# A two-layer encoder trunk on one core: the second layer's output projection in seven half-depth products, and six plain tiles at the start

## The chip, the cores and the metric

The kernel runs on one core of one Trainium2 chip. The metric is the device time of one execution in microseconds (us). A kernel is timed several times, and the median is given. Profiles come from one profiled execution, which has a time of its own.

## The reference

The input x is 2048 positions by 1024 channels in float32. The first (even) layer projects the normalised x to 6144 channels, makes a short convolution branch and a recurrent branch (RG-LRU, both directions) from them, and projects back. The second (odd) layer is a gated linear attention (GLA) with four heads, in both directions. The end of it is what the change touches:

```
h = rmsnorm(x, norm_pre)
q, k, v, r, lr = split(h @ w_in)
o = gla(q, k, v, g) + flip(gla(flip(q), flip(k), flip(v), flip(g_b)))   # 4 heads of 256 values
o = rmsnorm(o, head_norm_g)                                             # over each head's 256 values
y = (o * silu(r)) @ w_out                                               # 1024 x 1024
x = x + rmsnorm(y, norm_post)
```

## The kernel before, in words

Activations lie transposed: channels on the 128 partitions, positions along a row. The 2048 positions are cut into four chunks of 512 (CH). A product in near float32 accuracy takes three float16 matmuls: each operand is split into a high half (a copy to float16, on ACT) and a low half (operand minus high half, on DVE), and weight high times operand high, weight high times operand low and weight low times operand high are added up in PSUM. These are the three lines that stand together everywhere: 774 to 776 for the first layer's input projection, 1103 to 1105 for its output projection, 1492 to 1494 for the second layer's input projection, 2034 to 2036 for the second layer's output projection. The helpers act (line 250), stt (254) and tt (258) issue all the work of ACT and DVE, and dma (279) issues every DMA from SP's queue, in order.

*Seven products.* A product over depth 256 for 256 outputs can be made from seven products over half the depth and for half the outputs, in place of eight, from sums of operands made ahead (Strassen's scheme in Winograd's form). The kernel uses this for most of the first layer's input projection (two weight tiles as a pair, with operands H and with weights that DVE combines and splits) and for the second layer's input projection. In the first layer, the tiles in the list `first` are computed plainly, eight half-depth parts each, because the combined operands aren't there yet at the start; all others are in `pairs`.

*The order of the work.* The kernel is written as generators, "threads", which a planner (class Order, line 56) steps through while the program is built. Each step says which engine it uses and how long it should take; the planner keeps a clock for each engine, tile pools with caps, and priorities, and appends the instructions to each engine in the order that its clocks give. The chip then runs each engine's list strictly in that order. A change of a cost, a cap or a priority so moves many instructions. SBUF is kept in 23 slots of 8 KB a partition, with a cap for each role (H, YC, WO2, YC2, ZB and so on), PSUM in eight banks.

*The first stage.* x is loaded and normed (line 508 holds its ones product, which sums over partitions), the weights arrive in raw tiles, are split or combined (wsplit, line 429) into pieces, and PE works through `first` and then `pairs`. Beside it DVE makes the convolution of the recurrent branch in UA and splits it into UH, which the gate products (lines 944 to 946) read.

*The end of the second layer.* The GLA goes head by head (scores, states and outputs, lines 1797 to 1891). Behind each head, gpost norms its output o by chunks in the order 1, 2, 0, 3 (CORD): ACT squares, DVE adds, a ones product (line 456) sums, and the root is taken. The gate silu(r), made by ACT into DQ and kept in DRAM as rd, is loaded into YL, and gpost_out (line 1959) multiplies. High and low halves of y go to DRAM as yod, 256 KB each, and come back as YC2 tiles of four such pieces (yc2_loader, line 2013). The weights odd_wo come at the end as raw tiles of 512 KB and are split by wq_split (line 1998) into WO2. bg_wq (line 2038) then computes the projection for five blocks (three of 512 positions and two of 256): for each of eight groups of 128 outputs, eight parts of the depth, three matmuls each. For the first block four banks are filled side by side, one depth part after another, since operands arrive one by one. post_odd (line 2086) norms each block, adds x (ZX) and writes it out. In the trace the buffer numbers are left out, and both kinds of WO and YC tiles carry the names WO and YC.

Of the kernel before, what the change touches and what calls it, by code (L numbers as in the profile page):

```python
# [13 lines left out]
ALU = mybir.AluOpType  # L14
# [143 lines left out]
def trunk_kernel(ctx: ExitStack, tc: tile.TileContext, xT, w_in, gate_w, w_out, odd_w, lr_w, lr_gw, odd_wo, params, outT):  # L158
# [12 lines left out]
    S.pool("raw", ["raw0", "raw1", "hv0", "hv1"])  # L171
# [4 lines left out]
        XC=8, TMP=2, H=NH, PC=2, XA=1, UA=1, UH=1, R=1, I=1, T=3, A=1, G=2, U=3, Z=2, YH=1,  # L176
        WO=8, YC=6, YB=2, XR=4, H2=3, LM=1, WV=4, V=2, VD=2, XS=1, QS=2, E=4, SB=1, O=2, DQ=2, YL=2,
        WO2=4, YC2=4, ZB=2, ZX=2))
# [152 lines left out]
    def lam_consts():  # L331
# [23 lines left out]
        nc.vector.tensor_scalar(out=gsc[:, 8:16], in0=par[:, C_OPOST:C_OPOST + 8], scalar1=-2.0 ** -25, scalar2=None,  # L355
# [15 lines left out]
    def w_loader(items):  # L371
        for key, src in items:
            w = W[key]
            w.raw = yield from wget("raw", [128, 8, 128], F32)
            yield from dma(w.raw.t, src, 512 * 1024)
            done(w.evr)
# [220 lines left out]
    first = [("xa", 0), ("gc", 0), ("xb", 0), ("zb", 0)]  # L597
    pairs = [(("gb", 0), ("xa", 1))]
# [13 lines left out]
    for c in range(1, 7):  # L612
        GWAFT[("xa", c + 1)] = [c + 1]
    ev_proj = Ev()

    def even_loader():
        for i, key in enumerate(order):
# [6 lines left out]
            for c in GWAFT.get(key, ()):  # L624
                w = W["gw", c]
                w.raw = yield from wget("raw", [128, 512], F32)
                yield from dma(w.raw.t, gate_w[c], 256 * 1024)
                done(w.evr)

# [36 lines left out]
    def w_split_pairs():  # L666
        for pair in pairs:
# [27 lines left out]
            for key in pair:  # L695
                yield from gw_split(key)
        retire()
# [145 lines left out]
    def bg_even():  # L843
        bs, evs = [], []
        for key in first:
# [5 lines left out]
        for p in range(2):  # L851
            for i, key, hf in [(i, key, hf) for i, key in enumerate(first) for hf in range(2)]:
# [5 lines left out]
                if p == 1 and hf == 1:  # L858
                    done(evs[i])
        for c in range(1, NCH):  # L860
# [197 lines left out]
    def wo_loader():  # L1058
        for ki in range(16):
            WR[ki] = yield from wget("raw", [128, 1024], F32)  # L1060
            r0 = krow(ki)
            yield from dma(WR[ki].t, w_out[r0:r0 + 128, :], 512 * 1024)
            done(evWR[ki])
# [230 lines left out]
    for key, _ in items_odd:  # L1294
        W[key] = Wt()
    WU = {}
# [27 lines left out]
    def w_prep():  # L1324
# [13 lines left out]
        done(evLRP)  # L1338
        for u in UNITS:
            prs = ukeys(u)  # L1340
            for i, pr in enumerate(prs):
                ra, rb = W[pr[0]], W[pr[1]]
                tmp = yield from pget()
                s = f32(tmp)

                evo = [Ev() for _ in range(7)]

                def op(j, src, evo=evo, u=u, i=i, last=i == len(prs) - 1):
                    p = yield from pget()
                    yield from wsplit(p, src)  # L1350
                    S.spawn(w_save(u, j, i, p, last), 3)
                    done(evo[j])

                def close(ra=ra, rb=rb, evo=evo):
                    yield ("w", evo[0])
                    yield ("w", evo[4])
                    wput(ra.raw)
                    yield ("w", evo[5])
                    yield ("w", evo[6])
                    wput(rb.raw)  # L1360

                yield ("w", ra.evr)
                yield ("w", rb.evr)
                a11, a12 = ra.raw.t[:, 0:4], ra.raw.t[:, 4:8]
                a21, a22 = rb.raw.t[:, 0:4], rb.raw.t[:, 4:8]
                S.spawn(op(0, a11), 3)
                S.spawn(op(2, a12), 3)
                yield from tt(s, a21, a22, ALU.add)
                S.spawn(op(1, s), 3)
                S.spawn(op(5, a22), 3)  # L1370
                yield from tt(a21, a11, a21, ALU.subtract)
                S.spawn(op(6, a21), 3)
                yield ("w", evo[1])
                yield from tt(s, s, a11, ALU.subtract)
                S.spawn(op(3, s), 3)
                yield ("w", evo[2])
                yield from tt(a12, a12, s, ALU.subtract)
                S.spawn(op(4, a12), 3)
                S.spawn(close(), 3)
                yield ("w", evo[3])  # L1380
                pput(tmp)
            if u == UNITS[0]:
# [10 lines left out]
                done(evWZd)  # L1393
        done(evPrep)

    evPrep = Ev()
    evRaw = Ev()

    def w_save(u, j, i, p, last):
        d = wu_d[u, j]  # L1400
        yield from dma(d[:, :, :, i * 128:i * 128 + 128] if u[0] == "v" else d, p.t, 256 * 1024)
        pput(p)
        if last:
            done(evWD[u, j])
# [356 lines left out]
    def gla(hd):  # L1761
# [3 lines left out]
        yield ("w", evWVd)  # L1765
        xs = yield from get("XS", [128, 16, 128])
# [4 lines left out]
        sfb = yield from get("SB", [128, 8, 256])  # L1771
        O[hd] = o
# [143 lines left out]
    evPost = [Ev() for _ in range(4)]  # L1916

# [36 lines left out]
    def y_out(i, c, sl, y, yl):  # L1954
        yield from dma(yo_d[i][:, :, sl], y, 256 * 1024)
        count(("yl", i // 2, c), 2, lambda: put(yl))
        done(evYO[i, c])

    def gpost_out(hd, o, tp, evR, evG, YL, evYL):
        for p, c in enumerate(CORD):  # L1960
# [3 lines left out]
            yv = YL[c].t[:, 1024:2048].bitcast(F16).rearrange("p (e a t) -> p e a t", e=2, a=2)  # L1964
            for et in range(2):
                i = 2 * hd + et
# [6 lines left out]
                y = yv[:, et]  # L1973
                yield from act(y[:, 0], ot, AF.Copy, scale=16.0)
                yield from stt(y[:, 1], ot, 16.0, y[:, 0], ALU.mult, ALU.subtract)
                S.spawn(y_out(i, c, sl, y, YL[c]), 1)
        wput(tp)
        for s in o:
            put(s)
# [238 lines left out]
```

## Time and profile before

| | before |
|---|---|
| median of 3 | 2230.99 us (2228.64 to 2232.93) |
| the profiled execution | 2228.18 us |
| its span | 2226.4 us |
| mean granted TensorE clock | 0.989 |
| PE / DVE / ACT busy | 2142.4 / 1518.4 / 1254.4 us |
| moved by DMA | 443.88 MB, 199 GB/s over the span |

The span runs from the first instruction to the last; the execution's own time is 1.8 us longer. PE is TensorE's matmuls, PEld its weight loads, DVE, ACT and SP the vector, scalar and sync engines; POOL does next to nothing here. A row of a timeline gives the start, the duration, the engine, the line, the instruction, its output and inputs, and in brackets the time that the engine idled before it with what it waited for. The duration of a matmul covers its way through the array; the distance between two starts is what it costs.

### The profile page before, as it was taken

To read this page: it belongs to the slowest core of one execution; us is meant where nothing else is said; L and a number is where in the kernel's file an instruction comes from. 1 tells how busy PE (TensorE), PEld (TensorE's weight loads), DVE (VectorE), ACT (ScalarE), POOL (GpSimd) and SP (SyncE) were. 2 spreads that over 40 slices of the span, in tenths; PEclk is the share of its full clock that TensorE was granted. 3 is DMA by queue.
4 is the path that set the end of the run, shared out by engine and by line. 5 is a ranking of instruction groups with operands and counts; after the bars stand their busy time and mean duration, and the time that the engine had idled before them with its cause. 6 is when DMAs were issued, how large, how long until landed. Compare 5 with 4: busy or idle time off the path is not lost.

```text
span 2226.4 us, 27957 instructions
## 1 busy us (share of the span) xinstructions
PE 2142.4 (96%) x11290; PEld 1151.8 (52%) x11290; DVE 1518.4 (68%) x1720; ACT 1254.4 (56%) x1636; POOL 2.8 (0%) x8
## 2 busy tenths in 40 slices
PE   5979999999999999999999999999999999997997
PEld 4434444444444444444444444778566666674446
DVE  7987887888687777774476775766447475667435
ACT  5557776877777675663443334376355555655322
POOL 0000000000000000000000000000000000000000
PEclk9999999999999999999999999999999999998999
DMA  7354443543544545469566576256746667456533
GB/s 266 147 222 175 173 181 147 194 186 136 223 152 180 203 151 205 164 242 334 175 183 218 191 287 235 115 207 247 275 179 235 252 223 297 172 188 219 170 112 114
DMA packets 155057, 443.88 MB, mean 199 GB/s; under 512 B 39856, under 2 KB 76848, under 8 KB 121136
## 3 DMA queue, kind: packets, MB, share of 16 engines
q1 hardware_dynamic: 154928, 442.10, 54.4%
q8 instruction: 88, 1.44, 0.3%
q14 instruction: 41, 0.34, 0.0%
HBM read 325.40 MB, written 116.65 MB: 199 GB/s over the span
## 4 chain that ended last, share of the span: by engine, by line
PE 78%; DVE 10%; DMA 6%; ACT 3%; issue 2%; SPq 1%; DVEq 0%; ACTq 0%
PE ps L774 15%; PE ps L776 15%; PE ps L775 15%; PE ps L1103 3%; PE ps L1104 3%; PE ps L1105 3%; PE ps L2034 2%; PE ps L2036 2%; PE ps L2035 2%; PE ps L1829 2%; PE ps L1492 2%; PE ps L1494 2%; PE ps L1493 2%; DVE H L258 2%; DMA raw<-odd_w 1%
## 5 line engine op out<-in xcount | busy, mean ns | idle before, releaser
L774 PE MATMUL ps<-H,hl 128*128 128x512 f16 (+1 forms) x896 | 337.5, 377 | 14.2 <-ACT H L250 5.2
L775 PE MATMUL ps<-H,hl 128*128 128x512 f16 (+1 forms) x896 | 337.4, 377 | 4.3 <-DVE H L258 4.3
L776 PE MATMUL ps<-H,hl 128*128 128x512 f16 (+1 forms) x896 | 337.3, 376 | 3.9 <-DVE hl L254 3.7
L774 PE MATMUL ps<-H,PC 128*128 128x512 f16 (+1 forms) x752 | 283.4, 377 | 4.2 <-DMA H<-hd 3.2
L776 PE MATMUL ps<-H,PC 128*128 128x512 f16 (+1 forms) x752 | 283.3, 377 | 0.6 <-DVE PC L254 0.6
L775 PE MATMUL ps<-H,PC 128*128 128x512 f16 (+1 forms) x752 | 283.3, 377 | 0.0
L1103 PE MATMUL ps<-YC,WO 128*128 128x512 f16 x512 | 194.9, 381 | 0.0
L1104 PE MATMUL ps<-YC,WO 128*128 128x512 f16 x512 | 194.8, 380 | 0.0
L1105 PE MATMUL ps<-YC,WO 128*128 128x512 f16 x512 | 194.6, 380 | 0.0
L775 PEld LDWEIGHTS <-hl 128*128 128x128 f16 x896 | 88.4, 99 | 113.2 <-issue 15.0
L776 PEld LDWEIGHTS <-hl 128*128 128x128 f16 x896 | 88.4, 99 | 112.0 <-issue 7.0
L774 PEld LDWEIGHTS <-hl 128*128 128x128 f16 x896 | 88.5, 99 | 103.3 <-issue 3.9
L1492 PE MATMUL ps<-WV,H 128*128 128x256 f16 x448 | 122.1, 273 | 1.8 <-ACT VD L250 1.8
L1493 PE MATMUL ps<-WV,H 128*128 128x256 f16 x448 | 122.1, 273 | 0.0
L1494 PE MATMUL ps<-WV,H 128*128 128x256 f16 x448 | 122.1, 273 | 0.0
L774 PEld LDWEIGHTS <-PC 128*128 128x128 f16 x752 | 73.6, 98 | 93.3 <-DMA H<-hd 6.6
L2034 PE MATMUL ps<-YC,WO 128*128 128x512 f16 (+1 forms) x320 | 110.0, 344 | 10.5 <-DMA YC<-yod 10.5
L776 PEld LDWEIGHTS <-PC 128*128 128x128 f16 x752 | 73.6, 98 | 87.9 <-DVE PC L254 0.9
L775 PEld LDWEIGHTS <-PC 128*128 128x128 f16 x752 | 73.6, 98 | 86.8 <-issue 0.3
L150 ACT ACT_TABLE_LOAD x89 | 114.2, 1283 | 1.6
L2036 PE MATMUL ps<-YC,WO 128*128 128x512 f16 (+1 forms) x320 | 110.2, 344 | 0.0
L2035 PE MATMUL ps<-YC,WO 128*128 128x512 f16 (+1 forms) x320 | 109.8, 343 | 0.0
(234 smaller groups left out, 4159.5 us busy)
## 6 DMA issues: line engine op xcount, KB each, us to landing
H<-hd SPq DMA_DIRECT2D x112, 1024.0 KB, 6.1
H<-gd SPq DMA_DIRECT2D x56, 1024.0 KB, 8.9
raw<-w_in SPq DMA_DIRECT2D x48, 512.0 KB, 4.4
yd<-YH SPq DMA_DIRECT2D x16, 1024.0 KB, 4.9
YC<-yd SPq DMA_DIRECT2D x64, 256.0 KB, 5.7
hd<-H SPq DMA_DIRECT2D x14, 1024.0 KB, 5.5
gd<-H SPq DMA_DIRECT2D x14, 1024.0 KB, 4.7
raw<-odd_w SPq DMA_DIRECT2D x24, 512.0 KB, 5.2
```

The lines of the kernel that those rows point to most:

```text
L774: nc.tensor.matmul(b.t[:, sl], lhsT=wh, rhs=hi, start=s, stop=False, skip_group_check=True)
L775: nc.tensor.matmul(b.t[:, sl], lhsT=wh, rhs=lo, start=False, stop=False, skip_group_check=True)
L776: nc.tensor.matmul(b.t[:, sl], lhsT=wl, rhs=hi, start=False, stop=e, skip_group_check=True)
L1103: nc.tensor.matmul(b.t, lhsT=wh, rhs=hi, start=start, stop=False)
L1104: nc.tensor.matmul(b.t, lhsT=wh, rhs=lo, start=False, stop=False)
L1105: nc.tensor.matmul(b.t, lhsT=wl, rhs=hi, start=False, stop=stop)
L1492: nc.tensor.matmul(b.t[:, i], lhsT=hi, rhs=wh, start=st, stop=False, skip_group_check=True)
L1493: nc.tensor.matmul(b.t[:, i], lhsT=hi, rhs=wl, start=False, stop=False, skip_group_check=True)
L1494: nc.tensor.matmul(b.t[:, i], lhsT=lo, rhs=wh, start=False, stop=e, skip_group_check=True)
L2034: nc.tensor.matmul(out, lhsT=wh, rhs=hi, start=start, stop=False)
L2035: nc.tensor.matmul(out, lhsT=wh, rhs=lo, start=False, stop=False)
L2036: nc.tensor.matmul(out, lhsT=wl, rhs=hi, start=False, stop=stop)
```

## The change

Four things are changed.

1. **First stage.** `first` has six tiles, with ("gb", 0) and ("xa", 1) added, and `pairs` one pair fewer. The raw pool has a third tile, and loads of weights are issued without waiting for the one before to land.
2. **Weights of the last projection.** odd_wo is loaded in the first stage, two row blocks at a time (a head's 256 rows), behind four of the pairs. `prep` makes eight operands of each: seven for the seven products and one that the plain products need. They are split as other weights are and saved to DRAM (wq_d, eight tensors of 1 MB). Before head 3's GLA outputs, wq_loader loads them, one into each of eight WO2 slots.
3. **Operands.** y_ops makes the seven operands of each head and chunk from y (four for chunk 3), high and low halves of 128 by 256 each, in place in the YL tile. Those of heads 0 to 2 go to DRAM as one tensor for a head and chunk (128 by 3584 in float16; 128 by 2048 for chunk 3) and come back into YC2 slots. Those of head 3 stay in the YL tile, which the products read.
4. **Products.** Three chunks of 512 are computed by wq_seven: seven products, each for two pairs of output groups, four heads of depth, 256 columns. The first of them begins with products 0 to 2 of heads 0 to 2; head 3's part of these follows, then products 3 to 6. ACT and DVE add the results up into ZB. The last chunk is computed plainly from the operands that are halves of y and of the weights themselves. The blocks' norms and outputs are separate threads.

```
-    first = [("xa", 0), ("gc", 0), ("xb", 0), ("zb", 0)]
-    pairs = [(("gb", 0), ("xa", 1))]
+    first = [("xa", 0), ("gc", 0), ("xb", 0), ("zb", 0), ("gb", 0), ("xa", 1)]
+    pairs = []
...
-        WO2=4, YC2=4, ZB=2, ZX=2))
+        WO2=8, YC2=3, ZB=4, ZX=2))
...
+    WOAFT = {pairs[6 + 3 * h][1]: [h] for h in range(4)}
...
+                for hd in WOAFT.get(key, ()):
+                    yield from prep(W["wo", 2 * hd], W["wo", 2 * hd + 1], save_q(hd), True)
...
+    def prep(ra, rb, save, out=False):
+        tmp = yield from pget()
+        s = f32(tmp)
...
+        def op(j, src):
+            p = yield from pget()
+            yield from wsplit(p, src)
+            S.spawn(save(j, p), 3)
+            done(evo[j])
...
+    def y_ops(hd, c, o, yl):
...
+        def split(j, src):
+            yield from act(yv[:, j, 0], src, AF.Copy, scale=4.0)
+            yield from stt(yv[:, j, 1], src, 4.0, yv[:, j, 0], ALU.mult, ALU.subtract)
+            done(ev[j])
...
+        if hd == 3:
+            YC2[c, 3] = yl
+            done(evYC2[c, 3])
+        else:
+            S.spawn(y_out(hd, c, yl), 1)
...
     def wq_loader():
+        yield ("w", evGet3)
+        for j in range(8):
+            yield ("w", evWQd[j])
+            WQ[j] = yield from get("WO2", [128, 4, 2, 512], F16)
+            S.spawn(fetch(WQ[j].t, wq_d[j], 2 ** 20, evWQ[j]), 4)
...
     def yc2_loader():
+        yield ("w", evGet3)
+        for c in CORD:
+            for h in range(3):
+                yield ("w", evYO[h, c])
+                s = yield from get("YC2", [128, T])
...
+        def product(j, mb, hs):
...
+            yield ("w", evWQ[j])
+            for h in hs:
+                yield ("w", evYC2[c, h])
...
+            for i in range(2):
+                for h in hs:
+                    wq3(bk[b, mb].t[:, i], j, h, 2 * mb + i, yop(c, h, j), new and h == 0 and i == 0, h == 3)
...
+        if blk == 0:
+            for j in range(3):
+                for mb in range(2):
+                    yield from product(j, mb, (0, 1, 2))
+            for j in range(3):
+                for mb in range(2):
+                    yield from product(j, mb, (3,))
+        for j in range(3 if blk == 0 else 0, 7):
+            for mb in range(2):
+                yield from product(j, mb, (0, 1, 2, 3))
```

wq3 issues the three matmuls (lines 2096 to 2098 of the changed kernel), yop picks operand j of a head.

The change also moves instructions, since the planner places everything anew. On DVE in the first stage, before the change, UH (the low half of the convolved input, UA) stands at row 119 of DVE's list, and the first gate product at row 1015 of PE's, where a matmul and a weight load have a row each. H holds the operands of the input projection, XC is x.

```order
L258 TENSOR_TENSOR XC_420<-XC_481,XC_420 128x2048
L254 SCALAR_TENSOR_TENSOR UA_1011<-XA_253,par,UA_1011 128x2046
L258 TENSOR_TENSOR H_1042<-XC_420,H_1042 128x4x512
L254 SCALAR_TENSOR_TENSOR UA_1011<-XA_253,par,UA_1011 128x2047
L258 TENSOR_TENSOR H_1061<-XC_443,H_1061 128x4x512
L254 SCALAR_TENSOR_TENSOR UA_1011<-XA_253,par,UA_1011 128x2047
L258 TENSOR_TENSOR U_259<-U_259,G_256 128x2048
L254 SCALAR_TENSOR_TENSOR UH_1096<-UA_1011,UH_1096 128x2048
```

In the changed kernel the same place on DVE reads as follows; hl and raw are weights.

```order
L258 TENSOR_TENSOR H_1095<-XC_436,H_1095 128x4x512
L258 TENSOR_TENSOR H_1125<-XC_459,H_1125 128x4x512
L258 TENSOR_TENSOR hl_265<-raw_630 128x512
L254 SCALAR_TENSOR_TENSOR UA_1183<-XA_269,par,UA_1183 128x2046
L254 SCALAR_TENSOR_TENSOR UA_1183<-XA_269,par,UA_1183 128x2047 x2
L254 SCALAR_TENSOR_TENSOR hl_265<-raw_598,hl_265 128x512
L254 SCALAR_TENSOR_TENSOR UH_1217<-UA_1183,UH_1217 128x2048
```

UH is now at row 120 of DVE's list, and the first gate product at row 1255 of PE's, 120 matmuls and as many weight loads later.

On PE at the passage from head 3's GLA to the projection, before the change, the last outputs of the GLA (lines 1889 and 1891) are followed by the projection (YC and WO).

```order
L1889 MATMUL ps_15053<-XS_14490,V_14309 128x128
L1891 MATMUL ps_15053<-E_14304,SB_14493 128x128
L2034 LDWEIGHTS WO_1403_15074
L2034 MATMUL ps_14995<-YC_1402_15073,WO_1403_15074 128x512
L2035 LDWEIGHTS WO_1403_15074
L2035 MATMUL ps_14995<-YC_1402_15073,WO_1403_15074 128x512
```

In the changed kernel three pieces of the same passage are these: the last GLA outputs (lines 1924 and 1926) and a product of heads 0 to 2 behind them; the ones product (line 455) of head 3's second chunk, which stands among such products; and the first product that reads head 3's YL.

```order
L1924 MATMUL ps_15400<-XS_14725,V_14571 128x128
L1926 MATMUL ps_15400<-E_14566,SB_14728 128x128
...
L2098 MATMUL ps_15424<-YC_1333_14859,WO_1337_14918 128x256
L455 MATMUL ps_15403<-hv_15416,ones_r 128x512 x2
L2096 LDWEIGHTS WO_1337_14918
L2096 MATMUL ps_15450<-YC_1325_14800,WO_1337_14918 128x256
...
L2098 MATMUL ps_15450<-YC_1333_14859,WO_1337_14918 128x256
L2096 LDWEIGHTS WO_1334_14885
L2096 MATMUL ps_14989<-YL_15264,WO_1334_14885 128x256
```

The six products of heads 0 to 2 stand at rows 18297 to 18557 of PE's list, between parts of head 3's GLA, and the ones product of head 3's first chunk at row 18395, ahead of the last GLA outputs.

On SP, where the last loads before the second block of the projection stand, before the change the operands come in pieces of 256 KB, mixed with stores of head 3's y.

```order
L279 DMA yod_248<-YL_15135 256x1x512
L279 DMA YC_1422_15262<-yod_241 128x2x512
L279 DMA yod_247<-YL_15198 256x1x512
L279 DMA YC_1422_15262<-yod_242 128x2x512
L279 DMA yod_248<-YL_15198 256x1x512
L279 DMA YC_1422_15262<-yod_243 128x2x512
L279 DMA YC_1422_15262<-yod_244 128x2x512
```

In the changed kernel the same place has the last two weight loads (WO from wqd), the gates of head 3 for two chunks (YL from rd) and then the second block's operands (YC from yod), three tensors, one for each of heads 0 to 2.

```order
L279 DMA WO_1346_14991<-wqd_144 128x4096
L279 DMA WO_1347_14992<-wqd_145 128x4096
L279 DMA YL_15264<-rd_231 128x2x512
L279 DMA YL_15267<-rd_232 128x2x512
L279 DMA YL_15425<-rd_231 128x2x512
L279 DMA YL_15453<-rd_232 128x2x512
L279 DMA YC_1427_15801<-yod_251 128x3584
L279 DMA YC_1429_15803<-yod_255 128x3584
L279 DMA YC_1430_15804<-yod_259 128x3584
```

YC_1427 takes the slot of YC_1325, which the first block's products read up to PE's row 18997, and YC_1429 another slot that is read up to row 19015, the block's last matmul. On PE that matmul, the ones product of this block's norm and the second block's first matmul follow each other.

```order
L2098 MATMUL ps_15233<-YL_15264,WO_1346_14991 128x256
L455 MATMUL ps_15834<-hv_15828,ones_r 128x512 x2
L2096 LDWEIGHTS WO_1334_14885
L2096 MATMUL ps_15802<-YC_1427_15801,WO_1334_14885 128x256
L2097 LDWEIGHTS WO_1334_14885
L2097 MATMUL ps_15802<-YC_1427_15801,WO_1334_14885 128x256
```

Nothing else stands on PE between the two blocks.

More of the change, by code (lines that the diff above doesn't have):

```diff
@@ L859, in bg_even @@
                     done(evs[i])
+        for key in first[4:]:
+            yield from plain(key, 0)
         for c in range(1, NCH):
@@ L1295, in trunk_kernel @@
         W[key] = Wt()
+    wq_d = [drams.tile([128, 4, 2, 512], F16, tag=f"wq{j}", name=f"wqd{j}") for j in range(8)]
+    evWQd = [Ev() for _ in range(8)]
     WU = {}
@@ L1338, in w_prep, with save_u, save @@
         done(evLRP)
+        def save_u(u, i, last):
+            def save(j, p):
+                d = wu_d[u, j]
+                yield from dma(d[:, :, :, i * 128:i * 128 + 128] if u[0] == "v" else d, p.t, 256 * 1024)
+                pput(p)
+                if last:
+                    done(evWD[u, j])
+            return save
         for u in UNITS:
@@ L1341, in w_prep @@
             for i, pr in enumerate(prs):
[L1342 to L1381, printed above, removed]
+                yield from prep(W[pr[0]], W[pr[1]], save_u(u, i, i == len(prs) - 1))
             if u == UNITS[0]:
@@ L1972, in gpost_out @@
                 yield from tt(ot, g, ot, ALU.mult)
[L1973 to L1976, printed above, removed]
+            S.spawn(y_ops(hd, c, o, YL[c]), 2)
         wput(tp)
-        for s in o:
-            put(s)
+        if hd == 3:
+            S.pools["slot"]["caps"].update(YC2=6)
         done(evPost[hd])
-    yo_d = [drams.tile([128, 2, T], F16, tag=f"yo{i}", name=f"yod{i}") for i in range(8)]
@@ L1983, in trunk_kernel @@
-    evYO = {(i, c): Ev() for i in range(8) for c in range(NCH)}
+    yo_d = [[drams.tile([128, 2 * T], F16, tag=f"yo{h}{c}", name=f"yod{h}{c}") for c in range(NCH)] for h in range(4)]
+    evYO = {(h, c): Ev() for h in range(4) for c in range(NCH)}
     WQ = {}
     evWQ = [Ev() for _ in range(8)]
-    WQR = {}
-    evWQR = [Ev() for _ in range(8)]
     def wq_loader():
-        yield ("w", evRaw)
-        for k in range(8):
-            WQR[k] = yield from wget("raw", [128, 1024], F32)
-            yield from dma(WQR[k].t, odd_wo[k * 128:(k + 1) * 128, :], 512 * 1024)
-            done(evWQR[k])
@@ new lines, in yop, with wq3 @@
+    def yop(c, h, j):
+        return YC2[c, h].t.bitcast(F16).rearrange("p (j a t) -> p j a t", j=8, a=2)[:, j]
+    BLK = [(512, 512), (1024, 512), (0, 512), (1536, 256), (1792, 256)]
+    evF = {(b, m): Ev() for b in range(len(BLK)) for m in range(8)}
+    FB = {}
+    def wq3(out, j, h, m, y, start, stop):
+        wh, wl = [WQ[j].t[:, h, a, m * 128:(m + 1) * 128] for a in range(2)]
+        hi, lo = y[:, 0], y[:, 1]
+        nc.tensor.matmul(out, lhsT=wh, rhs=hi, start=start, stop=False, skip_group_check=True)
+        nc.tensor.matmul(out, lhsT=wh, rhs=lo, start=False, stop=False, skip_group_check=True)
+        nc.tensor.matmul(out, lhsT=wl, rhs=hi, start=False, stop=stop, skip_group_check=True)
@@ L2038, in bg_wq, with zb_get @@
+    ZB = {}
+    evZB = [Ev() for _ in range(len(BLK))]
+    def zb_get():
+        yield ("w", evGLA[3])
+        for blk, (t0, n) in enumerate(BLK):
+            ZB[blk] = []
+            for _ in range(2):
+                s = yield from get("ZB", [128, 4, n])
+                ZB[blk].append(s)
+            done(evZB[blk])
     def bg_wq():
@@ L2112, in post_odd, with out_dma @@
-            put(tmp)
+                for k in range(4):
+                    yield from stt(x[:, k], y[:, k], gsc[:, 8 + hf * 4 + k:9 + hf * 4 + k], x[:, k], ALU.mult, ALU.add)
+            else:
+                yield from tt(x, x, y, ALU.add)
+            S.spawn(out_dma(blk, hf, x), 0)
+            put(yb[hf])
+        put(tmp)
+    def out_dma(blk, hf, x):
+        t0, n = BLK[blk]
+        c = t0 // CH
+        yield from dma(outT[hf * 4:hf * 4 + 4, :, t0:t0 + n].rearrange("k p t -> p k t"), x, 2048 * n)
+        count(("zx", c, hf), CH // n, lambda: put(ZX[c, hf]))
```

295 lines of the change are left out of this document (186 added, 109 removed).

## The prediction, made before the run

> **What bounds the kernel now.** I read the page first, for the engines' shares and the costliest groups.
>
> ```profile
> PE 2142.4 (96%) x11290; PEld 1151.8 (52%) x11290; DVE 1518.4 (68%) x1720; ACT 1254.4 (56%) x1636; POOL 2.8 (0%) x8
> ...
> L2034 PE MATMUL ps<-YC,WO 128*128 128x512 f16 (+1 forms) x320 | 110.0, 344 | 10.5 <-DMA YC<-yod 10.5
> ```
>
> PE is busy for 2142.4 of 2226.4 us, so all its idle time is 84.0 us, and whatever gains more than that must take away matmuls. The busy time by stage says where the 84 lie. The columns are the stretch, its length, then busy time (and count) of PE, weight loads, DVE, ACT and POOL, the granted clock, the DMA share and GB/s.
>
> ```profile
> 0.00:56.00 56.00, 31.75 (x213) 22.93 (x214) 41.92 (x64) 33.15 (x38) 0.79 (x6) 0.94 0.73 264
> 56.00:112.00 56.00, 53.72 (x240) 24.16 (x240) 55.73 (x45) 31.01 (x29) 0.00 (x0) 1.00 0.37 151
> 112.00:168.00 56.00, 42.88 (x191) 18.73 (x189) 47.45 (x69) 31.00 (x37) 0.00 (x0) 0.91 0.56 217
> 168.00:1000.00 832.00, 831.67 (x3853) 376.75 (x3852) 644.88 (x629) 593.85 (x652) 0.00 (x0) 1.00 0.48 180
> ...
> 2020.00:2040.00 20.00, 13.10 (x63) 7.82 (x62) 13.44 (x24) 12.22 (x20) 0.00 (x0) 0.83 0.77 252
> 2040.00:2060.00 20.00, 14.63 (x50) 5.95 (x50) 19.42 (x27) 12.31 (x18) 0.00 (x0) 0.84 0.80 260
> 2060.00:2200.00 140.00, 140.00 (x780) 76.42 (x779) 58.90 (x61) 40.31 (x75) 0.00 (x0) 1.00 0.41 141
> 2200.00:2226.40 26.40, 14.18 (x124) 12.05 (x121) 15.09 (x21) 7.23 (x20) 0.00 (x0) 0.83 0.23 80
> ```
>
> From 168 to 1000 PE idles 0.33 us: only fewer matmuls help there. Idle time stands in the first 56 us (24.3), from 56 to 168 (2.3 + 13.1 = 15.4), from 2020 to 2060 (6.9 + 5.4 = 12.3), at the end (12.2), and the other 19.5 in small pieces between 1000 and 2020. PE's waits name the large ones (total, times, longest):
>
> ```profile
> PE ps L508 <- DVE TMP L258: 11.6, 1, 11.6
> PE ps L2034 <- DMA YC<-yod: 10.5, 3, 6.3
> PE ps L944 <- ACT UH L250: 10.1, 1, 10.1
> ```
>
> The first is the first layer's norm, which the change leaves alone. The second is the start of the projection that it rewrites. The third is the first gate product, waiting for UH, the convolved input, behind DVE's queue: DVE is full there, and PE is not.
>
> ```profile
> 130.00:140.00 10.00, 1.32 (x3) 0.36 (x3) 10.00 (x6) 4.79 (x3) 0.00 (x0) 0.59 0.97 369
> ```
>
> **The change part by part.** The profiled execution took 2228.18 us for the span of 2226.4, 2.8 under the median of 2230.99; the sum goes against it, and the difference is then applied to the median.
>
> *Six plain tiles.* Two tiles of four chunks in full take 2 × 4 × 8 × 3 = 192 matmuls of 512 columns, and as a pair in seven half-depth products 168: 24 more. Where they go matters more. The rows of order put the first gate product 120 matmuls later than before. PE waits and resumes there as follows:
>
> ```profile
> 136.85 0.59 PE L944 MATMUL ps<-UH,PC 128*128 128x512 f16 x1 [10.12 <-ACT UH L250]
> 139.27 0.59 PE L945 MATMUL ps<-UH,PC 128*128 128x512 f16 x1 [1.83 <-DVE UH L254]
> ...
> 142.09 0.38 PE L946 MATMUL ps<-UH,PC 128*128 128x512 f16 x1
> ```
>
> A matmul of 512 columns starts every 0.216 us at full clock, and one of 256 every 0.109, with a fresh weight load for each (second block):
>
> ```profile
> 2170.27 0.38 PE L2036 MATMUL ps<-YC,WO 128*128 128x512 f16 x1
> 2170.49 0.27 PE L2034 MATMUL ps<-YC,WO 128*128 128x256 f16 x1
> 2170.59 0.27 PE L2035 MATMUL ps<-YC,WO 128*128 128x256 f16 x1
> ```
>
> ```profile
> 2170.49 0.10 PEld L2035 LDWEIGHTS <-WO 128*128 128x128 f16 x1
> ```
>
> So 120 × 0.216 = 25.9 us of work now stand ahead of the gate, against 15.4 us idle from 56 to 168. DVE's list of instructions up to UH is about as long as before (119 rows before it, 120 now), so UH stays where it was (136.85 to 139.27, in two halves); PE, which was held 10.1 and 1.8 us there, now gets there around 139.3 − 12 + 25.9 = 153 and finds it done. The idle goes: −15.4. The slow clock behind it goes too: seven matmuls took 139.27 to 142.09, 2.82 us, where 7 × 0.216 = 1.5 would do: −1.3. Work: 24 × 0.216 = +5.2. Sum **−11.5**. Between ends: if half of the gaps stay, −4; nothing beyond −16, the work being left out.
>
> *Weights split in the first stage.* Four heads' preparations put 4 × 4 sums and 4 × 8 low halves on DVE and 32 high halves on ACT, all of 512 columns; eight DMAs into DRAM per head. The nearest rows by size, from the groups between 2020 and 2062 (busy, mean ns):
>
> ```profile
> L254 DVE SCALAR_TENSOR_TENSOR WO<-raw,WO 128x1024 f16<-128x1024 f32 x7 | 8.5, 1218 | 0.0
> ...
> L254 DVE SCALAR_TENSOR_TENSOR YL<-QS,YL 128x512 f16<-128x512 f32 x6 | 4.1, 684 | 0.0
> ```
>
> 48 × 0.684 = 33 us of DVE; ACT takes 0.69 for 512 columns (a row below), 32 × 0.69 = 22 us. From 168 to 1000 DVE has 832 − 645 = 187 us free and ACT 238. I take 0; if all the DVE work came through, +33 (a rival). What leaves the end: eight low halves of 1.218 us on DVE, 9.7 us in the stretch where DVE was busy 19.42 of 20.
>
> *Fewer matmuls.* Before: 192 of 512 and 128 of 256 columns on each of three lines, 768 in units of 512. After: three chunks take 7 products × 4 output blocks × 4 heads × 3 lines, 336 matmuls of 256 columns each, and the last chunk 384 as before: 1392, or 696 units. 72 × 0.216 = **−15.5**.
>
> *The transition into the projection.* Before:
>
> ```profile
> 2025.77 5.13 DMA YC<-yod
> 2030.95 0.58 PE ps L2034
> ...
> 2036.22 0.61 PE ps L456 x2
> ```
>
> PE waits 6.3 us for the first operands, and then the 12 matmuls to 2036.22 run at half rate: 5.27 us instead of 2.59, 2.7 lost. From 2030.95 to the first 256-wide matmul at 2170.49 are 139.5 us, for 576 × 0.216 = 124.3: 15.2 more, of which some 2.6 are ones products, and the rest waits and slow clock. With the first wait the transition costs 6.3 + 12.6 = 19.
>
> After: the products of heads 0 to 2 stand inside head 3's GLA, 6 × 18 × 0.109 = 11.8 us of cover. What is late next is head 3's own post chain:
>
> ```profile
> 2019.81 0.82 PE L456 MATMUL ps<-hv,ones_r 128*128 128x512 f32 x2
> ...
> 2024.34 0.69 ACT L250 ACTIVATE hv<-ps,epsb 128x512 f32<-128x512 f32 x1
> ...
> 2031.31 0.68 DVE L254 SCALAR_TENSOR_TENSOR YL<-QS,YL 128x512 f16<-128x512 f32 x1
> ```
>
> From the ones product to the first finished low half are 12.2 us. By the order PE has some 7 to 9 us of work behind those ones before it needs that half, so it waits about 5 us, then about 2 for the later operands (seven now, where there were two), with 2 to 2.5 of slow clock. 9.5 for 19: **−9.5**. Between −19 (all hidden) and 0. The gate loads of head 3 now stand in SP's queue behind seven 1 MB weight loads: 7.3 MB at the 369 GB/s of the row above are 20 us. By the order their issue lies about as far ahead of the need; if it lies less far, the wait grows.
>
> *The new wait.* The second block's operands of heads 0 to 2 go into the slots of the first block's, and all others are taken. The first of three loads waits for the last product that reads its slot, 18 matmuls (2 us) before the block ends; the second, for the block's last matmul; the third is queued behind it on SP, as are all later loads and outputs. Block 1's first product needs all three.
>
> ```profile
> H<-gd SPq DMA_DIRECT2D x56, 1024.0 KB, 8.9
> ...
> wdr<-hl SPq DMA_DIRECT2D x28, 256.0 KB, 2.1
> ```
>
> Three times 128 × 3584 × 2 bytes are 2.75 MB: 7.5 us at 369 GB/s, and about 1.4 us of latency (2.1 us for 256 KB, less 0.7 of transfer). With 2 us of lead and 0.6 of issue, PE idles 7 to 8 us; by 1024 KB rows that land in 8.9 us, 10. Beside it the ones product of block 0's norm is put before block 1, and PE waits for two sums, two squares and their additions behind the last matmul: by the rows above, about 2 × 0.68 + 1.05 + 1.22 + 3 × 0.65 = 6 us when DVE has no backlog. I take 8 idle, and 2.7 of slow clock as behind the wait of 6.3: **+10.7**; ends 0 (something covers it) and +15 (DVE behind, see below).
>
> [...]
>
> The end (12.2 us idle in the last stretch) keeps its form: 0. The early fetches, the larger raw pool and the output DMA issued apart: 0, covered by the 0.33 us of idle in the main stage; ±3 for the 19.5 us of small waits after 1000, which fall anew with each order.
>
> Sum: −11.5 − 15.5 − 9.5 + 10.7 = **−25.8**: 2202.4 against the profiled 2228.2, and 2205 against the median.
>
> **The rivals.**
>
> *The stop between blocks is covered* or under 3 us: −36, so 2195. For: the first load has a lead, and a PE that was held up inside block 0 gives DVE time to be done with the norm's earlier parts. Against: nothing else stands on PE between the blocks, and two of three loads wait for its last matmul. Chance 0.15.
>
> *The transition gives nothing.* Gate loads or DVE are late, and PE waits for the first head-3 operands as long as before, or block 0's last operands push the stop to 15: −26 + 9.5 + 4 = −12, so 2219. For: DVE was busy 19.42 of 20 us there and gets fourteen halves per chunk, some 30 us of work within block 0's second part, which lasts 26; the seven weight loads. Against: 9.7 us of weight splits left it. Chance 0.17.
>
> *Slower: the preparations starve the first stage.* They stand in line with the weight splits that feed PE and use the same pieces. One costs DVE 12 × 0.684 = 8.2 us; if each stops PE for that long, 4 × 8.2 = +33, so 2238. From 25.8 / 4 = 6.5 us a head on, the change is a loss. For: DVE was full up to 140 us. Against: the preparations come later, where DVE has 187 us free and PE waited 0.33 us in 832. Chance 0.05.
>
> *Slower: narrow matmuls wait for their weights.* The three chunks have 3 × 336 = 1008 of them: 1008 × (spacing − 0.109): from 25.8 / 1008 = 0.026 us each, a spacing of 0.135, it is a loss; with the whole 0.10 us of a load, +100, so 2305. Against: the rows at 2170 to 2171 have exactly this form and step by 0.10 to 0.11 with the loads beside. Chance 0.02. [...]
>
> **How the numbers follow.** The forecast, 2205, has 0.61 by itself, with ends 2196 to 2213 from its terms. The range, 2188 to 2219, takes in the first two rivals and the outer ends of the terms; outside lie the two slower rivals (0.07) and sums of several ends (0.12). A measurement here can tell 0.2%, 4.5 us. Faster, under 2226.5, are the forecast, the first rival and most of the second: 0.61 + 0.15 + 0.14 = 0.90. Same: the other 0.03 of the second, where half of the first stage's gain fails as well. Slower: 0.07.
>
> **What would show it.** Right: no gap over 2 us between 56 and 168 us, and the gate product at about 153; six products among head 3's GLA; one gap of 7 to 10 us some 40 us after head 3's first ones product, ended by a load into YC or by the norm's sums; the projection's matmuls 0.109 us apart. Wrong: gaps between 168 and 1000; spacing above 0.12; gaps for YL before the first head-3 product of over 8 us; no gap between blocks.

## The result, and the profile after

The changed kernel took 2200.15 us (median of 4 runs, 2196.99 to 2205.39), beside 2229.81 us for the kernel before on the same chip: a ratio of 0.9868 (95% interval 0.9845 to 0.989), 29.7 us less. The forecast was 2205, 25.8 less. The profiled execution took 2201.09 us with a span of 2199.2, where before it was 2226.4: 27.2 us less.

The page and the busy time by stage, with the columns as before:

```profile
PE 2131.1 (97%) x11746; PEld 1196.4 (54%) x11746; DVE 1576.2 (72%) x1894; ACT 1260.5 (57%) x1704; POOL 2.8 (0%) x8
```

```profile
0.00:56.00 56.00, 33.03 (x218) 23.67 (x219) 42.03 (x67) 34.02 (x40) 0.79 (x6) 0.94 0.82 287
56.00:112.00 56.00, 52.41 (x226) 22.96 (x225) 52.86 (x72) 29.00 (x27) 0.00 (x0) 0.97 0.35 142
112.00:168.00 56.00, 56.00 (x261) 25.34 (x260) 40.91 (x26) 29.02 (x32) 0.00 (x0) 1.00 0.30 113
168.00:1000.00 832.00, 831.78 (x3854) 376.92 (x3853) 679.12 (x681) 603.18 (x685) 0.00 (x0) 1.00 0.54 200
...
2020.00:2040.00 20.00, 19.45 (x173) 17.43 (x172) 17.98 (x37) 12.17 (x27) 0.00 (x0) 1.00 0.05 16
2040.00:2060.00 20.00, 18.09 (x156) 15.12 (x154) 16.89 (x34) 13.33 (x25) 0.00 (x0) 1.00 0.04 6
2060.00:2080.00 20.00, 13.14 (x99) 10.65 (x100) 15.78 (x24) 6.60 (x13) 0.00 (x0) 0.83 0.72 278
```

PE idles 2199.2 − 2131.1 = 68.1 us, 15.9 less than before. The idle time from 56 to 168 us fell from 15.4 to 3.6, that of the transition from 12.3 to under 2 (the last 0.6 before 2060 belong to the new stop; with the clock at 1.00 where it had been 0.83 and 0.84), and a new stop stands at 2060 to 2080: 6.9 us idle and a clock of 0.83. From 168 to 1000 PE still waits for nothing (0.2 us), though DVE has 34 us more to do.

PE's waits name the new ones: the norm's sums in the first stage (two waits now, where there was one) and the ones products, with four waits of which the stop is the longest:

```profile
PE ps L507 <- DVE TMP L258: 14.7, 2, 11.3
PE ps L455 <- ACT hv L250: 10.4, 4, 7.0
```

The new stop stands between the first and the second block of the projection. PE's timeline there:

```profile
2059.13 0.27 PE L2098 MATMUL ps<-YL,WO 128*128 128x256 f16 x1
2066.39 0.79 PE L455 MATMUL ps<-hv,ones_r 128*128 128x512 f32 x1 [6.98 <-ACT hv L250]
2067.65 0.80 PE L455 MATMUL ps<-hv,ones_r 128*128 128x512 f32 x1 [0.48 <-DVE hv L258]
2068.25 0.44 PE L2096 MATMUL ps<-YC,WO 128*128 128x256 f16 x1
```

The last product of the first block starts at 2059.13. PE then waits 7.0 + 0.5 us, and not for the second block's operands, as the forecast had it in the first place, but for the sums of the first block's norm; the operands (YC) follow at 2068.25 without a wait of their own. They came hardly earlier. The third and last of their loads is issued at 2059.87 and lands 7.9 us later, at 2067.8:

```profile
L279 SPq DMA_DIRECT2D YC<-yod x1: 424/424/424, 2059.9 to 2059.9; - x1
...
DMA to landing us min/median/max: 7.9/7.9/7.9
```

The DMA engines were full until 2068 (columns as above, stretches of 2, 1 and 2 us).

```profile
2064.00:2066.00 2.00, 0.00 (x0) 0.00 (x0) 1.97 (x3) 0.30 (x1) 0.00 (x0) 0.50 1.02 412
...
2067.00:2068.00 1.00, 0.52 (x2) 0.29 (x1) 1.00 (x3) 0.00 (x0) 0.00 (x0) 0.50 1.00 416
2068.00:2070.00 2.00, 2.00 (x10) 1.23 (x10) 1.93 (x4) 1.32 (x2) 0.00 (x0) 0.50 0.55 227
```

So two things end at about the same time, and only one of them is named by the waits. The experiments had to take them apart.

### The profile page after: what moved, and what is told of

Its sections match the earlier page's. It is cut to its first block, busy times and chain, and to the rows that moved or that the text cites. A ratio compares the mean times of both kernels' runs of the same rounds, so it can differ in the third digit from the quotient of the medians.

```text
span 2199.2 us, 29131 instructions
## 1 busy us (share of the span) xinstructions
PE 2131.1 (97%) x11746; PEld 1196.4 (54%) x11746; DVE 1576.2 (72%) x1894; ACT 1260.5 (57%) x1704; POOL 2.8 (0%) x8
## 4 chain that ended last, share of the span: by engine, by line
PE 74%; DVE 13%; DMA 6%; ACT 4%; issue 2%; SPq 1%; ACTq 0%; DVEq 0%
PE ps L785 15%; PE ps L787 15%; PE ps L786 15%; PE ps L1115 3%; PE ps L1116 3%; PE ps L1117 2%; PE ps L1864 2%; PE ps L2097 2%; PE ps L2096 2%; PE ps L2098 2%; DVE E L258 2%; DVE H L258 1%; PE ps L1832 1%; PE ps L957 1%; PE ps L959 1%
## 5 line engine op out<-in xcount | busy, mean ns | idle before, releaser
L785 PE MATMUL ps<-H,hl 128*128 128x512 f16 (+1 forms) x896 | 337.7, 377 | 15.5 <-ACT H L250 5.2
L785 PE MATMUL ps<-H,PC 128*128 128x512 f16 (+1 forms) x760 | 286.9, 377 | 3.5 <-DMA H<-hd 3.5
L787 PE MATMUL ps<-H,PC 128*128 128x512 f16 (+1 forms) x760 | 286.6, 377 | 0.5 <-DVE PC L254 0.5
L786 PE MATMUL ps<-H,PC 128*128 128x512 f16 (+1 forms) x760 | 286.7, 377 | 0.0
L250 ACT ACTIVATE hl<-raw 128x512 f16<-128x512 f32 x132 | 81.8, 629 | 73.6 <-DMA wdqk<-hl 20.5
L254 DVE SCALAR_TENSOR_TENSOR hl<-raw,hl 128x512 f16<-128x512 f32 (+1 forms) x132 | 89.1, 683 | 46.2 <-ACT hl L250 45.9
L258 DVE TENSOR_TENSOR SB<-ps,SB 128x256 f32<-128x256 f32 x112 | 46.4, 422 | 79.7 <-PE ps L1864 77.8
## 6 DMA issues: line engine op xcount, KB each, us to landing
H<-gd SPq DMA_DIRECT2D x56, 1024.0 KB, 10.7
```

What stands on the lines that cost most here:

```text
L254: nc.vector.scalar_tensor_tensor(out=out, in0=in0, scalar=scalar, in1=in1, op0=op0, op1=op1)
L258: nc.vector.tensor_tensor(out=out, in0=in0, in1=in1, op=op)
L785: nc.tensor.matmul(b.t[:, sl], lhsT=wh, rhs=hi, start=s, stop=False, skip_group_check=True)
L786: nc.tensor.matmul(b.t[:, sl], lhsT=wh, rhs=lo, start=False, stop=False, skip_group_check=True)
L787: nc.tensor.matmul(b.t[:, sl], lhsT=wl, rhs=hi, start=False, stop=e, skip_group_check=True)
```

## The experiments

The three runs on the stop, and the two on the transition behind them, share all code ahead of head 3's end with the changed kernel. The runs still differ by up to 8 us before that point, by waits and clock that fall differently from run to run, which is why I compare stretches inside the traces beside the ratios.

**The stop between the blocks: early_loads.** The second block's operands of heads 0 to 2 go to the six weight tiles (raw and hl) that are idle by then, as soon as head 3's first operands are there.

```
+        yield ("w", evYC2[CORD[0], 3])
+        for h in range(3):
+            yield ("w", evYO[h, c])
+            a = yield from wget("raw", [128, 4, 2, 256], F16)
+            b = yield from wget("hl", [128, 4, 2, 256], F16)
...
```

> Takes both waits at the border of the first two blocks away: the second block's operands of heads 0 to 2 are loaded into idle weight tiles before the first block ends, and the planner then puts the ones product of the first block's norm behind some products of the second block. The theory (loads and norm end at nearly the same time, each alone would hold PE): the 7.5 us of idle time and about 2 us of slow clock go, 9 us less than the changed kernel, near 2191. Rival (DVE's backlog is what counts): PE meets the same wait a few products later, for the sums that empty its banks or for the norm; 0 to 4 us less.

2189.79 us (4 runs); ratio to before 0.9811 (0.9798 to 0.9824), the best of all kernels here. PE's timeline at the border:

```profile
2054.69 0.27 PE L2116 MATMUL ps<-YL,WO 128*128 128x256 f16 x1
2054.80 0.27 PE L2114 MATMUL ps<-raw,WO 128*128 128x256 f16 x1
```

The second block starts 0.11 us after the last matmul of the first. The planner, which now has products to place, puts the norm's ones product behind three of them, and there PE waits 0.16 us for it.

**late_norm.** Only the ones product is moved, behind the second block's first four products.

```
+            if blk == 1 and j == 1 and mb == 1:
+                done(evLate)
...
+            if blk == 0:
+                yield ("w", evLate)
             b = yield from ones_mm2("fg", tmp.t[:, 0])
```

> Only the ones product of the first block's norm is put later, behind four products of the second block; the loads stay. The theory (loads and norm tie): PE then waits for YC by DMA until nearly the same time, under 1.5 us less than the changed kernel. Rival (the norm's chain alone holds PE, since the profile names only it): 8 us less. Rival (loads alone): no change.

2197.32 us (5 runs); ratio 0.9844 (0.9828 to 0.9861). PE's timeline shows the loads that had stood behind the norm:

```profile
2061.91 0.28 PE L2097 MATMUL ps<-YC,WO 128*128 128x256 f16 x1 [3.72 <-DMA YC<-yod]
2064.62 0.37 PE L2097 MATMUL ps<-YC,WO 128*128 128x256 f16 x1 [2.21 <-DMA YC<-yod]
2066.78 0.37 PE L2097 MATMUL ps<-YC,WO 128*128 128x256 f16 x1 [1.35 <-DMA YC<-yod]
```

3.72 + 2.21 + 1.35 = 7.3 us, one wait for each head's tensor, in place of the 7.5 for the norm.

**early_norm_first.** The early loads again, but the second block's products have to wait, in the planner's order, until the norm's ones product is placed.

```
+            if blk == 1:
+                yield ("w", evLate)
...
+            if blk == 0:
+                done(evLate)
```

> The second block's operands are loaded early, but its products wait, in the planner's order, until the ones product of the first block's norm is issued. The theory (tie) and the norm alone: the same wait of about 7 us for the norm's sums, within 1.5 us of the changed kernel. Rival (loads alone held PE): 8 us less.

2197.74 us (4 runs); ratio 0.9846 (0.9832 to 0.9859). The wait for the norm is back to the hundredth:

```profile
2058.51 0.79 PE L455 MATMUL ps<-hv,ones_r 128*128 128x512 f32 x1 [6.99 <-ACT hv L250]
```

From PE's wait of 0.55 us for YL, among the first products of head 3's operands, to the last ones product, the four traces have 154.4 us (the changed kernel, 2032.94 to 2187.32), 154.1 (late_norm), 155.6 (early_norm_first) and 145.0 (early_loads). Each wait alone holds PE for all of the time, and taking both away gives 9.4 us. The tie is shown; the profile's waits, read alone, would have put the cost on the norm. By their whole times late_norm and early_norm_first lie 2 to 3 us under the changed kernel (5 by the ratios, whose intervals overlap), more than the 1.5 expected; its own runs spread from 2197 to 2205.

**The transition: no_cover.** The first block's products take the four heads together.

```
-        if blk == 0:
-            for j in range(3):
-                for mb in range(2):
-                    yield from product(j, mb, (0, 1, 2))
...
+        for j in range(7):
```

> The first block no longer begins with the products of heads 0 to 2: all products take the four heads together, so that PE has nothing of the projection beside head 3's GLA. The theory (the gain of the transition is this cover, 11.8 us of products): 10 to 14 us more than the changed kernel, as a wait for YL at the first product. Rival (the gain came from the weights being split beforehand, and from DVE being free of it): 0 to 4 us more.

2208.9 us (4 runs); ratio 0.9897 (0.9884 to 0.9911), and a span 6.6 us longer. Between the last large wait for H and the last ones product stand 462.25 us in the changed kernel (1725.07 to 2187.32) and 470.68 here (1723.27 to 2193.95): 8.4 more. The cover is worth that, less than the 10 to 14 expected. The wait also has another place: not at a product that reads YL, but at head 3's second ones product, which now stands ahead of all products.

```profile
2022.43 0.80 PE L455 MATMUL ps<-hv,ones_r 128*128 128x512 f32 x1 [6.34 <-ACT hv L250]
```

**via_dram.** Head 3's operands go through DRAM, back into the same tile.

```
+            n = yn(c)
+            yield from dma(yo_d[3][c][:, 0:n], yl.t.bitcast(F16)[:, 0:n], 256 * n)
+            yield from dma(yl.t.bitcast(F16)[:, 0:n], yo_d[3][c][:, 0:n], 256 * n)
```

> Head 3's operands go to DRAM and back into the same tile before the products read them, as those of the other heads do. The theory (what remains of the transition is set by head 3's own chain, so that a round trip of about 10 us stands fully on PE's path): 8 to 13 us more than the changed kernel, as a wait by DMA for YL. Rival (the products of heads 0 to 2 leave enough cover): under 3 us.

2209.64 us (4 runs); ratio 0.9895 (0.9881 to 0.9908). The same stretch has 472.02 us (1722.57 to 2194.59), 9.8 more. Keeping the last head in SBUF pays what it saves of the round trip. Most of it is again waited for at a ones product, since the planner, seeing the gap, put head 3's third ones product ahead of the first product of YL:

```profile
2033.76 0.80 PE L455 MATMUL ps<-hv,ones_r 128*128 128x512 f32 x1 [7.08 <-ACT hv L250]
2035.09 0.80 PE L455 MATMUL ps<-hv,ones_r 128*128 128x512 f32 x1 [0.53 <-DVE hv L258]
2037.82 0.37 PE L2099 MATMUL ps<-YL,WO 128*128 128x256 f16 x1 [1.94 <-DMA YL<-yod]
```

**The first stage: four_tiles.** The changed kernel with the lists of before.

```
-    first = [("xa", 0), ("gc", 0), ("xb", 0), ("zb", 0), ("gb", 0), ("xa", 1)]
-    pairs = []
+    first = [("xa", 0), ("gc", 0), ("xb", 0), ("zb", 0)]
+    pairs = [(("gb", 0), ("xa", 1))]
...
-    WOAFT = {pairs[6 + 3 * h][1]: [h] for h in range(4)}
+    WOAFT = {pairs[7 + 3 * h][1]: [h] for h in range(4)}
```

> The changed kernel with four plain tiles at the start and one pair more, as before; the preparations stay behind the same pairs. The theory (six tiles put 26 us of products ahead of the gate, for which PE had waited): the wait for UH of about 10 us comes back, and the wait for the norm's sums at about 97 us goes; 6 to 9 us more than the changed kernel. Rival (the gain of the first stage came from the earlier fetches and the third raw tile): within 2 us of the changed kernel.

2209.76 us (4 runs); ratio 0.9897 (0.9884 to 0.9911); its span is 9.7 us longer. The wait for UH is back at its place, 10.11 us at 137.13, and the one at 97 us is gone. The six tiles are worth some 6 to 10 us in the changed kernel.

**six_tiles_alone.** The same lists put into the kernel before.

> The kernel before with nothing but the six plain tiles. The theory: idle time of 12 to 15 us goes from 56 to 168 us, 5.2 us of products come, and a wait at about 97 us with some slow clock takes back what it took in the changed kernel; 6 to 9 us less than before. Rival (the third raw tile is needed for it): within 3 us of before.

2237.61 us (11 runs); ratio 1.0021 (1.0011 to 1.0031): slower than before. The wait for UH is gone here too, but another comes:

```profile
231.05 0.58 PE L774 MATMUL ps<-H,PC 128*128 128x512 f16 x1 [11.94 <-ACT Z L250]
```

Something else in the change must keep that wait away. **six_raw3** gives the third raw tile to it, and **two_raw** takes it from the changed kernel.

> The kernel before with the six plain tiles and, beside them, the third raw tile of the change (and its smaller scratch). The theory (the wait of 11.9 us at 231 us, which the six tiles alone brought, is one for weights that come too late with two raw tiles): this wait goes, and 5 to 9 us less than before. Rival (the wait comes from where the planner puts the recurrence's instructions on ACT): it stays, within 3 us of the six tiles alone.

> The changed kernel without the third raw tile. The theory (raw tiles): a wait of about 12 us near 231 us comes back, 10 to 14 us more than the changed kernel. Rival (order on ACT, or the fetches that no longer wait for each other): within 3 us.

six_raw3: 2236.6 us (11 runs), ratio 1.0016 (1.0007 to 1.0024), with the wait of 11.94 us at 233 us. two_raw: 2201.03 us (4 runs), ratio 0.986 (0.9845 to 0.9875), without it. The raw tile does nothing here; that theory falls, twice.

Still left in the diff was a number that the prediction had passed over: the cap of XA, the slots for the recurrent branch's input, goes from 1 to 2. **six_xa2** is six_tiles_alone with that number.

```
-        XC=8, TMP=2, H=NH, PC=2, XA=1, UA=1, UH=1, R=1, I=1, T=3, A=1, G=2, U=3, Z=2, YH=1,
+        XC=8, TMP=2, H=NH, PC=2, XA=2, UA=1, UH=1, R=1, I=1, T=3, A=1, G=2, U=3, Z=2, YH=1,
```

> The kernel before with the six plain tiles and two slots in place of one for XA, the recurrent branch's input, as in the changed kernel. The theory (with six plain tiles the second tile of XA is ready early and holds PSUM banks until the first one's slot is free, which is behind the recurrence on ACT): the wait of 11.9 us at 231 us goes, 6 to 9 us less than before. Rival (order on ACT, whatever the slots): it stays, and the time is that of the six tiles alone, 3 to 5 us more than before.

2222.74 us (6 runs); ratio 0.9965 (0.9953 to 0.9977), 7.8 us less than before. No wait is left between 97 and 300 us. A tile that is computed earlier needs a place earlier. With one slot, the second tile, ("xa", 1), is first copied out of PSUM at 144.5 us, behind the convolution's read of the first at 139.5; with two it is at 65.5. At the wait of 11.94 us it is the tile after that one. ACT's rows, first of six_tiles_alone, then of six_xa2:

```profile
221.90 2.10 ACT L250 ACTIVATE UA<-XA,par 128x2048 f32<-128x2048 f32 x1
...
230.42 0.58 ACT L250 ACTIVATE Z<-ps 128x512 f32<-128x512 f32 x1
230.90 0.59 ACT L250 ACTIVATE XA<-ps 128x512 f32<-128x512 f32 x1
```

```profile
215.16 0.58 ACT L250 ACTIVATE XA<-ps 128x512 f32<-128x512 f32 x1
...
225.15 2.08 ACT L250 ACTIVATE UA<-XA,par 128x2048 f32<-128x2048 f32 x1
```

With one slot the copies that free PE's banks (Z and XA from ps) stand behind the read of XA (UA from XA); with two, XA's copy stands 10 us ahead of it.

**The preparations: double_prep.** Each operand of the last projection's weights is split twice.

> Each operand of the last projection's weights is split twice in the first stage, 32 more instructions on ACT and 32 on DVE, about 22 us each; nothing is computed otherwise. The theory (the preparations are hidden, DVE and ACT have room from 168 to 1000 us): within 2 us of the changed kernel. Rival (they stop PE): some of 22 us more, as gaps between 168 and 1000 us.

2218.38 us (5 runs); ratio 0.9942 (0.9927 to 0.9956): 16 us more than the changed kernel. The theory said that nothing would show, and is wrong. Two waits for weights stand behind the last of the four preparations:

```profile
824.99 0.61 PE L785 MATMUL ps<-H,hl 128*128 128x512 f16 x1 [8.09 <-ACT hl L250]
831.09 0.61 PE L787 MATMUL ps<-H,hl 128*128 128x512 f16 x1 [5.07 <-DVE hl L254]
```

The stretch ahead of them, first of this run and then of the changed kernel (third and fourth busy time: DVE, ACT):

```profile
800.00:820.00 20.00, 16.90 (x79) 7.45 (x77) 19.97 (x19) 17.59 (x21) 0.00 (x0) 1.00 0.17 68
```

```profile
800.00:820.00 20.00, 20.00 (x94) 9.05 (x93) 14.70 (x20) 15.73 (x16) 0.00 (x0) 1.00 0.70 266
```

DVE is full at 19.97 of 20. Room for 22 us is there over the whole stage, but not behind the fourth preparation, whose saves the changed kernel issues from 768 to 790 us. One set of splits is hidden, since PE has no wait over 0.22 us from 168 to 1000 in the changed kernel; two are not. Why it is the fourth that fails, and none of the three before it, was not tested.

**A chunk less in seven products: third_plain.**

```
-        return 4 * CH if c == CORD[3] else 7 * CH
+        return 4 * CH if c in CORD[2:] else 7 * CH
...
-    BLK = [(512, 512), (1024, 512), (0, 512), (1536, 256), (1792, 256)]
+    BLK = [(512, 512), (1024, 512), (0, 256), (256, 256), (1536, 256), (1792, 256)]
```

> The third chunk of the projection is computed plainly as the last one is: 48 matmuls of 256 columns more, three operands fewer to make, save and load for each head, and two more norms of 256. The theory (a seven-product chunk saves 48 matmuls of 0.109 us and the rest is hidden): 5.2 us more than the changed kernel, 4 to 7. Rival (the sums in ZB and the operands cost what the products save): within 2 us.

2221.56 us (5 runs); ratio 0.995 (0.9936 to 0.9965): 18 us more than the changed kernel, where 5.2 were expected. Its span is 17.5 us longer, 8.9 of them PE's busy time (5.2 of work; the other 3.7 were not taken apart) and 8.6 idle. One of the new waits is inside the projection:

```profile
2159.46 0.37 PE L2096 MATMUL ps<-YC,WO 128*128 128x256 f16 x1 [4.18 <-ACT ZB L250]
```

Another is a load of H at 1846 (4.0 us, 0.7 in the changed kernel). As a price for 48 matmuls the run is of no use: the planner placed the rest anew, and that cost more than the work. It does show that such a change can't be priced by its matmuls alone.

## Why the prediction was right, point by point

The forecast was −25.8, and the profiled execution has −27.2. Of its four terms two were off, in opposite directions; that the sum still came out near is in part luck.

*Fewer matmuls, −15.5: right.* Products of 256 columns start 0.109 us apart, from 2070.77 on as from 2170.49 before; the rival of narrow matmuls waiting for their weights is out. Weight loads are busy 17.4 of 20 us beside PE's 19.45 from 2020 to 2040, so the two overlapped here.

*Six plain tiles, −11.5: the size was off.* The gate's wait went, but a new one for the norm's sums came, seen in all runs with six tiles:

```profile
96.74 2.77 PE L507 MATMUL ps<-TMP,ones 128*128 128x512 f32 x4 [3.47 <-DVE TMP L258]
```

Idle time from 0 to 168 us fell by 13.1; with 5.2 of work and the slow clock behind the new wait (granted clock 0.97 from 56 to 112 us, before 1.00) replacing that behind the old (0.91 from 112 to 168 us, now 1.00), the term is −8, beside 7.8 less in six_xa2 and 6 to 10 more in four_tiles. The step that failed is "The idle goes: −15.4".

The wait for UH also went in another way than forecast. The step "so UH stays where it was" failed, though DVE's list up to it was as long as before:

```profile
139.30 0.60 ACT L250 ACTIVATE XA<-ps 128x512 f32<-128x512 f32 x1 [4.58 <-PE ps L787]
139.93 2.09 ACT L250 ACTIVATE UA<-XA,par 128x2048 f32<-128x2048 f32 x1
...
151.21 2.29 DVE L254 SCALAR_TENSOR_TENSOR UH<-UA,UH 128x2048 f16<-128x2048 f32 x1 [1.43 <-ACT UH L250]
...
154.64 0.38 PE L957 MATMUL ps<-UH,PC 128*128 128x512 f16 x1
```

The convolution starts at 139.93, where it was 114.04 before, since it reads the whole of XA, and XA's fourth piece now comes from PE at 139.30 in place of 107.96. So UH is done at 153.5, some 14 us later than before, and the first gate product at 154.64 finds it done by 1.1 us, where the prediction had counted on 14. That the wait is gone is to that extent luck.

And one condition was missing: without the second slot for XA the same six tiles cost 5 us. The prediction did not name the cover of that edit at all.

*The preparations, 0: right, but for a thinner reason than given.* "DVE has 187 us free" is a mean over 832 us; by double_prep the room where it counts is less than 22 us.

*The transition, −9.5: too small.* Idle time fell from 12.3 to under 2 and the clock stayed full (1.00). From head 3's first product at 2030.81 to the end of the block are 28.4 us, for 24.9 of matmuls (228 of 0.109 us) and some 1.3 of ones products: the 19 us of before are down to some 2.3, which makes −16.7. PE's timeline of the changed kernel:

```profile
2017.71 0.82 PE L455 MATMUL ps<-hv,ones_r 128*128 128x512 f32 x2
...
2032.94 0.27 PE L2097 MATMUL ps<-YL,WO 128*128 128x256 f16 x1 [0.55 <-DVE YL L254]
...
2044.58 0.51 PE L455 MATMUL ps<-hv,ones_r 128*128 128x512 f32 x1 [1.10 <-ACT hv L250]
```

The step that failed is "PE has some 7 to 9 us of work behind those ones before it needs that half". From 2017.71 the first product of YL is reached at 2030.81, 13.1 us later: four products of 18 matmuls each (7.9 us), the rest of the GLA and another ones product. DVE's first low half starts at 2028.96, 11.3 us after the ones product; before, it was 11.5 (2019.81 to 2031.31). The chain was read rightly and the cover counted too short. The gate loads were in time: no wait for them appears. no_cover (8.4 more) and via_dram (9.8 more) show that both parts of this edit are needed: with either gone, head 3's chain stands on PE's path. What the weights' splits, gone from this stage, add to the 16.7 was not tested by itself.

*The new wait, +10.7: right in size and place, with the norm's part too small.* From the last product's start at 2059.13 to 2070.77, where the matmuls are back at full rate, are 11.6 us. At full clock the work in them takes 2.3: 13 matmuls of 0.109 us, and 0.85 for two ones products, as at 2044.58. That makes +9.4, as much as early_loads gains: 7.5 idle and 1.9 of slow clock, where 2.7 was taken. The prediction put the loads first, with 7 to 8 us, and the norm beside them with 6; the runs show them level. PE stops at 2059.4; the third load lands 8.4 us later, and the norm's second ones product starts 8.2 us later. The norm's chain runs through DVE and ACT in turn, and DVE had head 3's operands (YL) in between:

```profile
2060.13 1.28 DVE L258 TENSOR_TENSOR ZB<-ps,ZB 128x512 f32<-128x512 f32 x2
...
2062.46 0.75 DVE L254 SCALAR_TENSOR_TENSOR YL<-QS,YL 128x256 f16<-128x256 f32 x2
2062.57 1.06 ACT L250 ACTIVATE TMP<-ZB 128x1024 f32<-128x1024 f32 x1 [2.11 <-DVE TMP L258]
...
2063.73 1.94 DVE L258 TENSOR_TENSOR TMP<-TMP 128x1024 f32<-128x1024 f32 x2
2065.59 0.69 DVE L258 TENSOR_TENSOR ps<-ps,hv 128x512 f32<-128x512 f32 x1
2065.70 0.63 ACT L250 ACTIVATE hv<-TMP 128x512 fp32r<-128x512 f32 x1 [2.07 <-DVE TMP L258]
```

−8 − 15.5 − 16.7 + 9.4 = −30.8, where −27.2 was measured. Of the remaining +3.6, 1.7 are slow clock behind one wait at 1537 us, which no other trace here has (see the last section); idle time from 1000 to 2020 is the same (19.6 before and 19.9 after). Runs with the same code there differ by as much, so I don't put it down to the change. What the other 1.9 are stays open.

## What to carry to other kernels

Where a wait has one name in the profile, ask what would end next: here a load and a norm ended within a microsecond of each other, only one was named, and in the same stretch of the trace removing either gained nothing while removing both gained 9.4 us. An earlier product needs its output's place earlier as well: six tiles with one slot lost 5 us and with two gained 8, so the caps of a pool belong to the edit's working as much as its instructions. And free time as a mean over a stage is no cover: 22 us more on DVE and ACT, with 187 free on DVE before, cost 16 us, most of it at one place. A wait that is gone can also be gone by little: UH came 14 us later than forecast, and 1.1 us ahead of its use.

## What the runs showed of the hardware

A wait of PE for about 2.4 us went either way for its clock. In the changed kernel the wait before one product of the second layer's input projection was 2.43 us, and the stretch from there to the wait at 1616 took 78.9 us; in third_plain it was 2.38 us, and the same stretch took 77.3, as in the other twelve traces, of which two_raw has a wait of 2.36 us there. From 1538 to 1541 the granted clock was 0.54 in the changed kernel and 1.00 in third_plain (0.21 and 0.11 us from one product's start to the next).

```profile
1537.36 0.27 PE L1523 MATMUL ps<-WV,H 128*128 128x256 f16 x1 [2.43 <-ACT VD L250]
...
1616.29 0.38 PE L785 MATMUL ps<-H,hl 128*128 128x512 f16 x1 [2.95 <-ACT QS L250]
```

```profile
1536.83 0.27 PE L1523 MATMUL ps<-WV,H 128*128 128x256 f16 x1 [2.38 <-ACT VD L250]
...
1614.08 0.58 PE L785 MATMUL ps<-H,hl 128*128 128x512 f16 x1 [2.95 <-ACT QS L250]
```

The wait of 2.95 us (2.94 in double_prep) that ends these stretches stands in all fourteen traces. The twelve matmuls from it on take 2.6 us in six_raw3 and six_xa2, and 3.9 to 4.3 in the others: the same wait cost nothing twice and 1.3 to 1.7 us of slow clock in the other twelve.

What decides which way a wait goes was not shown. By my estimate from these rows, up to 1.7 us at a single wait, this is one source of the spread of about 4 us on either side between runs of one kernel (2196.99 to 2205.39 us for the changed one).
